# A second norm's column sums by transposes and a VectorE sum, moved into the middle of a product

## The chip, the cores and the metric

The kernel runs on one core of a Trainium2 chip. A core has a matrix engine (TensorE, PE in the profile, with its weight loads shown as PEld), a vector engine (VectorE, DVE), an activation engine (ScalarE, ACT), GpSimd (POOL) and the queues that issue DMAs (SP, and those of ACT and POOL). Each engine takes its own instructions in order, and semaphores hold an instruction back until another engine has done its part. The metric is the device time of one execution in microseconds; less is better.

## The reference

One decoder layer on a sequence of 1024 positions with a width of 1024, all in float32. Cut to what matters here:

```python
def rmsnorm(x, gain):
    y = x * lax.rsqrt(jnp.mean(x * x, axis=-1, keepdims=True) + 1e-6)
    return y * gain

h = rmsnorm(x, mix_norm)                      # first norm: its scale is also needed by the attention
x = x + merged @ w_out                        # attention, spatial gating, gates, output projection
x = x + conv_gated_mlp(rmsnorm(x, ffn_norm), w_up, conv_w, conv_b, w_down)   # second norm
```

`conv_gated_mlp` multiplies by `w_up` (1024 x 5632), applies a causal convolution of width 3, gates one half with the other and multiplies by `w_down`.

## The kernel before

All activations lie with channels on the 128 partitions and positions along the free axis. Each float32 product is made of three products of a high and a low part (`mm3` at L92 to L94, `prod` at L1127): high by high, high by low, low by high. The large products are blocked by 2 x 2 and use seven block products in place of eight, with sums of weight and activation blocks; the block names (A11, S1, T4 ...) are those of that scheme. In the up-projection a `Pair` is one gate chunk and one value chunk of 128 channels; there are 22 pairs, each of seven products of 12 matmuls, and its result lies in two PSUM tiles, `zg` (halves `g0`, `g1`) and `zv` (halves `v0`, `v1`).

**The norm's scale.** The second norm's scale is not applied to its input but to the result of the first product, since it is one number per position. Its way is:

- `square` (L1554 on) squares the new residual on ScalarE and adds the eight channel chunks on GpSimd into `sq2`, 128 partitions by 1024 positions. Its last adds are those of L1567.
- `ssq_cols` (L1747) sums `sq2` over the partitions. For each of eight groups of 128 positions, `sq2` stands as the weights and a tile `ones` of two columns is streamed, so that the sums land with positions on the partitions, in columns of `pb`, which is the still unused `zv` tile of the next pair (`q2`). VectorE copies every other column to `ss8b` (128 x 8), multiplies by 1/1024 and adds epsilon (L130), and GpSimd raises it to the power -0.5 (L131).
- `rms_rows` (L135) makes rows of that column again: for each of the eight groups one column is broadcast as the weights, and the 128 x 128 identity `ident` is streamed, so that each partition gets the scale of every position. ScalarE copies the PSUM result to `rstd_b` (L143), and VectorE multiplies with it (`scale`, L1150).

`rms_rows` is used at two places: for the first norm in the first attention step (tile `rb`, about 43 to 45 us), and for the second norm inside the second pair (about 543 to 545 us). Each is eight matmuls in the program, which the profile shows as sixteen records: a float32 matmul is recorded twice.

**The order of the work.** TensorE's order is the order of the code, for the whole kernel (a manual schedule); from the phases named here on the other engines' order is also that of the code. `first_pair` (L1843 on) runs the seven products of pair 0, and ends in the product A22·T4 into `v0`, `ssq_cols`, and then splits and sums of the next pairs' weights on GpSimd and ScalarE (`split_s3`, `sum_s2`, `sum_s4`, `adds`, which issues two DMAs from GpSimd's queue, `split_q_half`). `fast_pair(1, ...)` begins with A11·B11 of pair 1, and behind it calls `rms`: the `rms_rows` of the second norm, the scaling of pair 0, and then pair 0's convolution.

Of the kernel before, what the change touches and what calls it, by code (L numbers as in the profile page):

```python
# [10 lines left out]
F = mybir.dt.float32  # L11
# [3 lines left out]
ALU = mybir.AluOpType  # L15
AX = mybir.AxisListType
# [17 lines left out]
def build(tc, a):  # L34
    nc = tc.nc
    ctx = ExitStack()
    with ctx, tc.manual_schedule(engines={mybir.EngineType.PE}):
        body(ctx, tc, nc, a)


def body(ctx, tc, nc, a):
    L, H = slice(0, 512), slice(512, 1024)
    base = ctx.enter_context(tc.tile_pool(name="base", bufs=1))
# [28 lines left out]
    def PS(s):  # L72
        if psum.get("next"):
            return psum["next"].pop(0).tile([128, 1024], F, tag="P", name=nm(s))
        pools_ = psum["P"]
        pools_.append(pools_.pop(0))
        return pools_[-1].tile([128, 1024], F, tag="P", name=nm(s))
# [36 lines left out]
    sink_b = base.tile([128, 8], F, name="sink_b")  # L114
    ident = base.tile([128, 128], F, name="ident")
    rstd_b = base.tile([128, 1024], F, name="rstd_b")
    ones = base.tile([128, 2], F, name="ones")
    mh05 = base.tile([128, 8], F, name="mh05")
    rstd = base.tile([128, 8], F, name="rstd")
    nc.gpsimd.memset(rstd_b[:, 0:128], 1.0)  # L120
    nc.gpsimd.memset(ones, 1.0)
    nc.gpsimd.memset(mh05, -0.5)
    g2 = cp[:, 0:8]
    ng2 = sink_b
# [3 lines left out]
    def rsqrt_cols(dst, ss, n, width):  # L128

        nc.vector.tensor_scalar(dst, ss, 1.0 / width, EPS, op0=ALU.mult, op1=ALU.add)  # L130
        return nc.gpsimd.tensor_tensor(dst, dst, mh05[:, :n], op=ALU.pow)  # L131
# [3 lines left out]
    def rms_rows(pb, col, hs=(0, 1)):  # L135

        for h, p in zip(hs, pb):
            for s in range(4):
                c = 4 * h + s
                nc.tensor.matmul(p[:, s * 128:(s + 1) * 128], col[:, c:c + 1].to_broadcast([128, 128]), ident,  # L140
                                 start=True, stop=True)
        for h, p in zip(hs, pb):
            nc.scalar.copy(rstd_b[:, h * 512:(h + 1) * 512], p)  # L143

# [526 lines left out]
    def sub(eng, out, x, y, op=ALU.subtract):  # L671
        eng.tensor_tensor(out, x, y, op=op)
        return out
# [24 lines left out]
    for n in range(20):  # L698
# [12 lines left out]
        if n == 0:  # L711
            for h in (0, 1):
                rms_rows([PH("rb")], rstd, (h,))
# [252 lines left out]
    pools = {"dr": dr}  # L966
# [147 lines left out]
    class Blocks:  # L1114
# [9 lines left out]
            if self.zv is not None:  # L1124
                self.v0, self.v1 = self.zv[:, L], self.zv[:, H]

        def prod(self, o, l, r, more=False):  # L1127
            (wh, wl), y, nk = self.w[l], self.y[r], self.nk
            for k in range(nk):
                for j, (p, q) in enumerate(((wh, 0), (wh, 1), (wl, 0))):  # L1130
                    m = y[:, q, k, :] if nk == 4 else y[:, 2 * q + k, :]
                    nc.tensor.matmul(o, p[:, k, :], m, start=not more and k == 0 and j == 0,  # L1132
                                     stop=k == nk - 1 and j == 2, skip_group_check=True)
# [386 lines left out]
    def right_split(n, e, src):  # L1520

        right_split_hi(n, e, src)
        right_split_lo(n, e, src)

    def right_split_hi(n, e, src):
        copy_hi(comb_tile(n)[:, 0, 2 * e:2 * e + 2, :], src)

    def right_split_lo(n, e, src):
        t = comb_tile(n)
        ds = slice(2 * e, 2 * e + 2)  # L1530
        nc.vector.tensor_tensor(t[:, 1, ds, :], src, t[:, 0, ds, :].bitcast(F), op=ALU.subtract)
# [9 lines left out]
    def gain(n, d):  # L1541
        k = 4 * (int(n[0]) - 1) + d
        return g2[:, k:k + 1], ng2[:, k:k + 1]
# [11 lines left out]
    def square(n, e):  # L1555

        q = pools["sq2"][:, (L, H)[int(n[1]) - 1]]
        if n == "21":
            t = ob[n][:, 2 * e:2 * e + 2, :]
        else:  # L1560
            t = pools["fp"].tile([128, 2, 512], F, tag="sqt", name=nm("sqt"))
        nc.scalar.activation(t, ob[n][:, 2 * e:2 * e + 2, :], AF.Square)
        if n in ("11", "12") and e == 0:
            nc.gpsimd.tensor_tensor(q, t[:, 0, :], t[:, 1, :], op=ALU.add)
        else:
            for k in (0, 1):
                nc.gpsimd.tensor_tensor(q, q, t[:, k, :], op=ALU.add)  # L1567

    def stt(out, x, g, y, op):
        nc.vector.scalar_tensor_tensor(out, x, g, y, op0=ALU.mult, op1=op)  # L1570
# [131 lines left out]
    def a22_split():  # L1702
        w0.split(("A22",), w0.q[:, 4:8], *(wst.tile([128, 8, 128], R, tag="w" + x, name=nm("q" + x))[:, 0:4] for x in "hl"))

    def fax_split():
        fx = pools["fp"].tile([128, 4, 512], R, tag="hA", name="fax")
        w0.split(("S2", "S4"), w0.r, *(fx[:, 2 * i:2 * i + 2, :].rearrange("p a (b m) -> p (a b) m", m=128)
                                       for i in (0, 1)))
# [37 lines left out]

    def ssq_cols(p):  # L1747
        for s in range(8):
            nc.tensor.matmul(p[:, 2 * s:2 * s + 2], pools["sq2"][:, s * 128:(s + 1) * 128], ones,
                             start=True, stop=True)  # L1750
        pool = pools["fp"]
        ss = pool.tile([128, 8], F, name="ss8b")
        nc.vector.tensor_copy(ss, p[:, 0:16].rearrange("p (s two) -> p s two", two=2)[:, :, 0])
        rsqrt_cols(ss, ss, 8, D)
        return ss

# [72 lines left out]
    def first_pair():  # L1829
        w, nx = lefts[0], lefts[1]  # L1830
        pools["mr_cm"].__exit__(None, None, None)
        pools["ex"] = ctx.enter_context(tc.tile_pool(name="ex", bufs=1, side="right", reuse_waits="tile"))
        z = PS("pz"), PS("pz")
        q, q2 = Pair(0, w.w, z[::-1]), Pair(1, nx.w)
        xu = pools["fp"].tile([128, 1024], F, tag="xu", name="xu")
        x7, u2 = xu[:, L], xu[:, H]
        x1 = pools["wx"].tile([128, 512], F, tag="x1f", name="x1f")

        q.prod(q.v1, "A11", "B11")
        a22_split()  # L1840
        nc.scalar.copy(x1, q.v1)
        fax_split()
        nx.load_p()  # L1843
        nx.load_q()
        nx.load_s3()
        q.prod(q.g1, "S1", "T1")
        for e in (0, 1):
            right_split_hi("T2", e, ob["B"][:, 2 * e:2 * e + 2, :])
        for e in (0, 1):
            right_split_lo("T2", e, ob["B"][:, 2 * e:2 * e + 2, :])  # L1850
        nc.scalar.copy(u2, q.g1)
        lefts[2].load_ahead()
        q.prod(q.v0, "S3", "T3")
        square("21", 0)
        nx.adds()
        square("21", 1)
        nc.scalar.copy(x7, q.v0)
        for e in (0, 1):
            for i in (0, 1):
                d = 2 * e + i  # L1860
                p = ob["X"][e][:, i, :]
                stt(p, p, gain("21", d)[0], ob["B"][:, d, :], ALU.add)
        for e in (0, 1):
            right_split("T4", e, ob["X"][e])
        q.prod(q.g1, "S4", "B22", more=True)
        q.prod(q.g0, "A12", "B21")
        nc.vector.tensor_tensor(q.g0, q.g0, x1, op=ALU.add)
        sub(nc.vector, x7, x7, u2)
        q.prod(q.v1, "S2", "T2", more=True)
        nx.split_p()  # L1870
        q.prod(q.v0, "A22", "T4", more=True)
        pb = q2.zv
        ratio = ssq_cols(pb)
        nx.split_s3()
        nx.sum_s2()
        nx.sum_s4()
        lefts[2].adds()
        nx.split_q_half(0)
        nx.split_q_half(1)
        lefts[2].load_p()  # L1880
        nc.scalar.copy(u2, q.v1)
        q.u2 = u2
        sub(nc.vector, q.v1, x7, u2)
        sub(nc.vector, q.v0, q.v0, u2)

        def rms():

            rms_rows([pb[:, L], pb[:, H]], ratio)
            q.scale(q.zv)
            q.last_sum()  # L1890

        pools["ft_cm"] = tc.tile_pool(name="ft", bufs=1, reuse_waits="tile")
        return q, q2, rms
# [82 lines left out]
    def mlp():  # L1976
# [200 lines left out]
        def start1():  # L2177
            prep(1)
            loads(3)

        prev, q, rms = first_pair()
        for n in range(1, NPAIR):
            q = fast_pair(n, prev, q or Pair(n, lefts[n].w), (start0, start1, start), rms)
# [119 lines left out]
```

## Time and profile before

| what | value |
| --- | --- |
| time, median of 3 runs | 1157.84 us (1157.07 to 1158.2) |
| the profiled execution, its own time | 1157.13 us |
| span of its trace | 1155.4 us |
| PE busy | 1150.4 us, 100% of the span, 5789 records |
| weight loads busy | 978.1 us, 85% |
| DVE busy | 857.0 us, 74% |
| ACT busy | 588.7 us, 51% |
| POOL busy | 658.3 us, 57% |

The span runs from the first to the last recorded instruction; the 1.7 us between it and the execution's own time lie before and behind. Matmuls overlap: one matmul's recorded duration is longer than the distance to the next one's start, so TensorE's pace is read from distances of starts or from the chain of waits, not from durations. In a row of the timeline stand the start in us, the duration in us, the engine, the line, the operation, the tiles written and read with their shapes, the count of instructions merged in it, and in brackets the idle time before it with what ended it.

### The profile page before, as it was taken

The page shows a single profiled execution, that of the slowest core. Times are in us where ns is not written, and L with a number is a line of the kernel's source. Part 1 is how long each engine was busy: PE and PEld are TensorE (multiplying, and loading weights), DVE is VectorE, ACT ScalarE, POOL GpSimd, SP SyncE. Part 2 cuts the span into 40 slices and gives each one's busy share as a digit, 9 for nine tenths or more (in the row PEclk, how much of TensorE's full clock was granted, in tenths as well). Part 3 has the DMA queues.
Part 4 walks back from the last instruction along what each step waited for, and adds up shares of the span by engine and source line. Part 5 has one row for each costly group of instructions (what it writes and reads, how often), then busy time and mean ns, then how long its engine had stood idle before and what let it go on. Part 6 is the DMA issues. An engine that isn't in the chain of part 4 may idle for free.

```text
span 1155.4 us, 15810 instructions
## 1 busy us (share of the span) xinstructions
PE 1150.4 (100%) x5789; PEld 978.1 (85%) x5789; DVE 857.0 (74%) x987; ACT 588.7 (51%) x896; POOL 658.3 (57%) x461
## 2 busy tenths in 40 slices
PE   9999999999999999999999999999999999999998
PEld 9999999888888888888888888888888888888887
DVE  7787747734436889887998978797788887766664
ACT  6665568643436546686444444444444354425231
POOL 1768674598783755798877676767676730000000
PEclk9999999999999999999999999999999999999999
DMA  9443565265747766644655554645464358966571
GB/s 367 149 147 67 137 217 201 74 209 174 202 108 240 240 213 237 191 143 120 165 166 149 152 137 137 173 129 145 131 171 134 111 201 308 353 220 197 176 229 56
DMA packets 86429, 204.37 MB, mean 177 GB/s; under 512 B 9616, under 2 KB 17296, under 8 KB 86160
## 3 DMA queue, kind: packets, MB, share of 16 engines
q1 hardware_dynamic: 77280, 174.93, 43.9%
q0 software_dynamic: 8544, 19.93, 10.4%
q10 hardware_dynamic: 528, 8.52, 2.1%
q8 instruction: 45, 0.74, 0.3%
q14 instruction: 32, 0.26, 0.1%
HBM read 162.70 MB, written 57.41 MB: 191 GB/s over the span
## 4 chain that ended last, share of the span: by engine, by line
PE 93%; POOL 3%; DMA 2%; DVE 1%; issue 1%; SPq 0%; ACT 0%; POOLq 0%
PE pz L1132 56%; PE pdx L2083 9%; PE pd L2083 8%; PE pY L1723 2%; PE pX L1723 2%; POOL wjl L1591 1%; PE pu L94 1%; PE pu L92 1%; PE pu L93 1%; PE pvs L94 1%; PE pvs L92 1%; PE pvs L93 1%; PE pv L568 1%; PE pq L92 1%; PE pq L93 1%; PE pq L94 1%
## 5 line engine op out<-in xcount | busy, mean ns | idle before, releaser
L1132 PE MATMUL pz<-T,qh 128*128 128x512 f32 x464 | 143.0, 389 | 0.0
L1132 PE MATMUL pz<-B,ph 128*128 128x512 f32 x352 | 108.6, 390 | 0.0
L1132 PEld LDWEIGHTS pz<-T,qh 128*128 128x128 f32 x464 | 87.0, 188 | 18.3 <-ACT u L949 0.3
L1084 POOL TENSOR_TENSOR pl<-lp,ph 128x1024 fp32r<-128x1024 f32 x30 | 73.3, 2443 | 37.0 <-ACT ph L88 37.0
L1132 PE MATMUL pz<-T,ql 128*128 128x512 f32 x232 | 90.3, 389 | 0.0
L1150 DVE TENSOR_TENSOR pz<-pz,rstd_b 128x1024 f32<-128x1024 f32 x60 | 73.9, 1232 | 6.1 <-ACT rstd_b L143 4.1
L1132 PEld LDWEIGHTS pz<-B,ph 128*128 128x128 f32 x352 | 65.9, 188 | 13.6
L1084 POOL TENSOR_TENSOR ql<-lq,qh 128x1024 fp32r<-128x1024 f32 (+1 forms) x31 | 76.4, 2488 | 0.0
L1132 PE MATMUL pz<-T,s3h 128*128 128x512 f32 x232 | 71.4, 389 | 0.0
L1132 PE MATMUL pz<-y,wjh 128*128 128x512 f32 x224 | 69.5, 391 | 0.1
L1132 PE MATMUL pz<-B,pl 128*128 128x512 f32 x176 | 68.6, 390 | 0.1
L88 ACT ACTIVATE qh<-lq 128x1024 fp32r<-128x1024 f32 (+1 forms) x31 | 31.5, 1020 | 69.3 <-POOL pl L1084 47.4
L1084 POOL TENSOR_TENSOR s3l<-lq,s3h 128x512 fp32r<-128x512 f32 x20 | 26.0, 1301 | 65.9 <-ACT s3h L88 65.9
L1372 POOL TENSOR_TENSOR wjl<-wj,wjh 128x512 fp32r<-128x512 f32 (+1 forms) x32 | 42.0, 1332 | 35.6 <-ACT wjh L88 29.8
L1132 PE MATMUL pz<-B,AX 128*128 128x512 f32 x252 | 60.6, 389 | 0.0
L1132 PE MATMUL pz<-T,AX 128*128 128x512 f32 x252 | 60.5, 389 | 0.0
L2083 PE MATMUL pdx<-bh,ah 128*128 128x512 f32 x152 | 59.2, 390 | 0.0
L2083 PE MATMUL pdx<-bh,al 128*128 128x512 f32 x152 | 59.1, 389 | 0.0
L2083 PE MATMUL pdx<-bl,ah 128*128 128x512 f32 x152 | 59.1, 389 | 0.0
L1144 ACT COPY u<-pz 128x512 f32<-128x512 f32 x28 | 16.4, 587 | 80.8 <-DVE pz L1143 80.8
L1771 DVE SCALAR_TENSOR_TENSOR tg<-pz,cp,tg 128x1023 f32<-128x1023 f32 (+1 forms) x44 | 56.2, 1278 | 0.8
L1771 DVE SCALAR_TENSOR_TENSOR tv<-pz,cp,tv 128x1023 f32<-128x1023 f32 (+1 forms) x44 | 56.2, 1278 | 0.8
(402 smaller groups left out, 3574.6 us busy)
## 6 DMA issues: line engine op xcount, KB each, us to landing
lp<-wup SPq DMA_DIRECT2D x22, 512.0 KB, 3.8
lq<-wup SPq DMA_DIRECT2D x22, 512.0 KB, 4.1
ra<-wdown SPq DMA_DIRECT2D x44, 256.0 KB, 4.5
b<-T SPq DMA_DIRECT2D x44, 256.0 KB, 3.7
lq<-wup POOLq DMA_DIRECT2D x42, 256.0 KB, 5.1
B<-tv SPq DMA_DIRECT2D x33, 256.0 KB, 2.3
T<-tt SPq DMA_DIRECT2D x33, 256.0 KB, 2.1
b<-B SPq DMA_DIRECT2D x33, 256.0 KB, 3.0
```

The lines of the kernel that those rows point to most:

```text
L88: return nc.scalar.activation(dst, src, AF.Copy, scale=scale)
L92: nc.tensor.matmul(out, wh, mh, start=first, stop=False, **kw)
L93: nc.tensor.matmul(out, wh, ml, start=False, stop=False, **kw)
L94: nc.tensor.matmul(out, wl, mh, start=False, stop=last, **kw)
L1084: nc.gpsimd.tensor_tensor(l, r, h.bitcast(F), op=ALU.subtract)
L1132: nc.tensor.matmul(o, p[:, k, :], m, start=not more and k == 0 and j == 0, stop=k == nk - 1 and j == 2, skip_group_check=True)
L1144: nc.scalar.copy(self.u2, self.v1)
L1150: nc.vector.tensor_tensor(z, z, rstd_b, op=ALU.mult)
L1372: nc.gpsimd.tensor_tensor(l[:, k], r[:, k], h[:, k].bitcast(F), op=ALU.subtract)
L1723: nc.tensor.matmul(ob[o][e][:, d, :], p[:, 4 * d + k, :], m[:, q, k, :], start=s in (0, 5) and k == 0 and i == 0, stop=k == 3 and i == 2, ...
L1771: nc.vector.scalar_tensor_tensor(t[:, j:], p[:, 0:1024 - j], cw[:, ci, 2 - j:3 - j], t[:, j:], op0=ALU.mult, op1=ALU.add)
L2083: nc.tensor.matmul(o[d], p[:, k - k0, m], q[:, k - k0, :], start=new and k == 0 and j == 0, stop=k == HK - 1 and j == 2, skip_group_check= ...
```

## The change

Three edits.

1. In `ssq_cols` the eight matmuls with two columns of ones become eight transposes with the identity: each brings a 128 x 128 piece of `sq2` to PSUM with positions on the partitions. All 1024 columns of `pb` are written. VectorE's copy becomes a sum over each group of 128 columns (`tensor_reduce`, 128 x 1024 in PSUM to 128 x 8). The tile `ones` and its memset on GpSimd are gone; a pad of the same size keeps the places of the other tiles.
2. In `rms_rows` the eight matmuls with the identity become eight transposes of the broadcast column, at both places.
3. `ssq_cols` is called in the middle of the product A22·T4: `prod` gets a list of chunks `ks`, the first two chunks (six matmuls) run before the transposes and the last two behind. VectorE's subtraction `x7 - u2` (tile `xu`) moves from ahead of the copy to behind the sum and its scaling.

```diff
-    ones = base.tile([128, 2], F, name="ones")
+    base.tile([128, 2], F, name="pad_b")
...
-    nc.gpsimd.memset(ones, 1.0)
...
         for h, p in zip(hs, pb):
             for s in range(4):
                 c = 4 * h + s
-                nc.tensor.matmul(p[:, s * 128:(s + 1) * 128], col[:, c:c + 1].to_broadcast([128, 128]), ident,
-                                 start=True, stop=True)
+                nc.tensor.transpose(p[:, s * 128:(s + 1) * 128], col[:, c:c + 1].to_broadcast([128, 128]), ident)
...
-        def prod(self, o, l, r, more=False):
+        def prod(self, o, l, r, more=False, ks=None):
             (wh, wl), y, nk = self.w[l], self.y[r], self.nk
-            for k in range(nk):
+            for k in ks or range(nk):
...
     def ssq_cols(p):
         for s in range(8):
-            nc.tensor.matmul(p[:, 2 * s:2 * s + 2], pools["sq2"][:, s * 128:(s + 1) * 128], ones,
-                             start=True, stop=True)
+            c = slice(s * 128, (s + 1) * 128)
+            nc.tensor.transpose(p[:, c], pools["sq2"][:, c], ident)
         pool = pools["fp"]
         ss = pool.tile([128, 8], F, name="ss8b")
-        nc.vector.tensor_copy(ss, p[:, 0:16].rearrange("p (s two) -> p s two", two=2)[:, :, 0])
+        nc.vector.tensor_reduce(ss, p.rearrange("p (s d) -> p s d", d=128), axis=AX.X, op=ALU.add)
         rsqrt_cols(ss, ss, 8, D)
...
-        sub(nc.vector, x7, x7, u2)
         q.prod(q.v1, "S2", "T2", more=True)
         nx.split_p()
-        q.prod(q.v0, "A22", "T4", more=True)
+        q.prod(q.v0, "A22", "T4", more=True, ks=(0, 1))
         pb = q2.zv
         ratio = ssq_cols(pb)
+        sub(nc.vector, x7, x7, u2)
+        q.prod(q.v0, "A22", "T4", more=True, ks=(2, 3))
```

The order on TensorE, at the end of pair 0 in `first_pair`. `pz` is a PSUM tile of a product, `T` the activation block T4, `qh` and `ql` the high and low weights of A22, `sq` is `sq2`, `B` with `ph` and `pl` the first product of pair 1. Before:

```order
L1132 MATMUL pz_5436<-T_702_5514,qh_5454 128x512 x2
L1132 MATMUL pz_5436<-T_702_5514,ql_5455 128x512
L1132 MATMUL pz_5436<-T_702_5514,qh_5454 128x512 x2
L1132 MATMUL pz_5436<-T_702_5514,ql_5455 128x512
L1132 MATMUL pz_5436<-T_702_5514,qh_5454 128x512 x2
L1132 MATMUL pz_5436<-T_702_5514,ql_5455 128x512
L1132 MATMUL pz_5436<-T_702_5514,qh_5454 128x512 x2
L1132 MATMUL pz_5436<-T_702_5514,ql_5455 128x512
L1749 MATMUL pz_5439<-ones,sq_4748 128x2 x8
L1132 MATMUL pz_5438<-B_659_5112,ph_5557 128x512 x2
```

Now (line numbers are lower by two from here on, and the tile numbers by one):

```order
L1130 MATMUL pz_5435<-T_702_5513,qh_5453 128x512 x2
L1130 MATMUL pz_5435<-T_702_5513,ql_5454 128x512
L1130 MATMUL pz_5435<-T_702_5513,qh_5453 128x512 x2
L1130 MATMUL pz_5435<-T_702_5513,ql_5454 128x512
L1748 MATMUL pz_5438<-ident,sq_4747 128x128 x8
L1130 MATMUL pz_5435<-T_702_5513,qh_5453 128x512 x2
L1130 MATMUL pz_5435<-T_702_5513,ql_5454 128x512
L1130 MATMUL pz_5435<-T_702_5513,qh_5453 128x512 x2
L1130 MATMUL pz_5435<-T_702_5513,ql_5454 128x512
L1130 MATMUL pz_5437<-B_659_5111,ph_5555 128x512 x2
```

The eight instructions on `sq2` stand six matmuls earlier than before, and stream 128 columns each in place of two.

The order on VectorE at the same place. `xu` holds `x7` and `u2`, `ss8b` is the column of sums, `pz_5439` (now `pz_5438`) is `pb`. Before:

```order
L1867 TENSOR_TENSOR pz_5437<-pz_5437,x1f 128x512
L672 TENSOR_TENSOR xu<-xu 128x512
L1753 COPY ss8b<-pz_5439 128x8
L130 TENSOR_SCALAR ss8b<-ss8b 128x8
L672 TENSOR_TENSOR pz_5436<-xu 128x512
L672 TENSOR_TENSOR pz_5436<-pz_5436,xu 128x512
L1150 TENSOR_TENSOR pz_5436<-pz_5436,rstd_b 128x1024
```

Now:

```order
L1865 TENSOR_TENSOR pz_5436<-pz_5436,x1f 128x512
L1751 TENSOR_REDUCE ss8b<-pz_5438 128x8
L129 TENSOR_SCALAR ss8b<-ss8b 128x8
L670 TENSOR_TENSOR xu<-xu 128x512
L670 TENSOR_TENSOR pz_5435<-xu 128x512
L670 TENSOR_TENSOR pz_5435<-pz_5435,xu 128x512
L1148 TENSOR_TENSOR pz_5435<-pz_5435,rstd_b 128x1024
```

The subtraction within `xu` stands behind the sum and its scaling, and the copy is a reduction. On ScalarE and on the SP queue nothing moves; on GpSimd only the memset of `ones` is gone, in the kernel's first rows.

## The prediction

> **What bounds the kernel now.** I read the page first: engines, then the granted clock.
>
> ```profile
> span 1155.4 us, 15810 instructions
> PE 1150.4 (100%) x5789; PEld 978.1 (85%) x5789; DVE 857.0 (74%) x987; ACT 588.7 (51%) x896; POOL 658.3 (57%) x461
> PEclk9999999999999999999999999999999999999999
> ```
>
> TensorE is busy for the whole span at the full clock, so time can come only out of TensorE's queue or out of its few waits. Next the chain of waits around the two places that the change touches (start, duration, what), and the busy time of two long stretches (start:end, length, then busy time of PE, PEld, DVE, ACT, POOL; clock, DMA).
>
> ```profile
> 43.90 1.78 PE rb L140 x16
> ...
> 59.08 0.44 PE pt L538 x4
> ...
> 535.85 2.72 PE pz L1132 x12
> 538.57 1.68 PE pz L1749 x16
> 540.25 2.89 PE pz L1132 x12
> 543.13 1.78 PE pz L140 x16
> 544.92 397.22 PE pz L1132 x1752
> ...
> 45.00:205.00 160.00, 160.00 (x1206) 151.15 (x1205) 110.41 (x219) 106.40 (x293) 108.09 (x115) 1.00 0.50 151
> 540.08:1152.00 611.92, 611.90 (x2715) 506.70 (x2714) 478.98 (x462) 264.73 (x304) 291.97 (x171) 1.00 0.56 171
> ```
>
> All three groups that are changed lie on the chain, and behind each TensorE goes on without a gap: 160.00 of 160.00 us, and 611.90 of 611.92. So a shorter group is a gain as long as no other engine falls behind. Where that is nearest is told by TensorE's waits between the two places (in total, times, longest):
>
> ```profile
> PEld pz L1132 <- POOL pl L1084: 0.5, 1, 0.5
> PEld pz L1132 <- ACT x L1392: 0.5, 2, 0.3
> PEld pz L1132 <- DVE y L1306: 0.5, 1, 0.5
> ```
>
> They are half a microsecond each, and what they wait for is itself fed by TensorE's results (the chain goes back from each of them to TensorE).
>
> **The change part by part.** *The price of a transpose.* The trace has float32 transposes of the same size: four of them (L538) take 0.44 us of the chain above, 0.11 each, and their 64 are recorded once each:
>
> ```profile
> L538 PE MATMUL pt<-ident,c x64: 270/272/273, 58.9 to 158.9; 128*128 128x128 f32 x64
> ```
>
> *`rms_rows`, two places.* Sixteen records, 1.78 us each time. Eight transposes at 0.11 are 0.88 us. TensorE gains 0.90 at each.
>
> *`ssq_cols`.* Sixteen records, 1.68 us; eight transposes are again 0.88, a gain of 0.80. Together TensorE's queue gets 0.90 + 0.80 + 0.90 = 2.60 us shorter. There is up to 0.17 more: the twelve matmuls ahead of the second `rms_rows` took 2.89, while those of A22 took 2.72, and part of that may be a wait for the power on GpSimd (below), which ended at 542.79 while the load that needs it began at 542.84. I leave this 0.17 to the range.
>
> The page "TensorE: Matmul & The Clock Gate" of the Trainium skill, Part 4, speaks against the edit: it gives about 275 ns for a transpose inside a kernel. The trace agrees with that as a recorded duration (272 ns), not as the distance at which transposes follow each other (110 ns); by the page's figure 24 transposes would be an estimated 6.6 us.
>
> *The DVE sum and the way to the scale.* What must be early is the scale's chain. These are its rows (timeline), with rows for the price of a reduction:
>
> ```profile
> 540.29 0.17 DVE L1753 COPY ss8b<-pz 128x8 f32<-128x8 f32 x1 [1.18 <-PE pz L1749]
> 540.49 0.17 DVE L130 TENSOR_SCALAR ss8b<-ss8b 128x8 f32<-128x8 f32 x1
> 540.57 0.69 DVE L672 TENSOR_TENSOR pz<-xu 128x512 f32<-128x512 f32 x1
> 540.74 2.05 POOL L131 TENSOR_TENSOR ss8b<-ss8b,mh 128x8 f32<-128x8 f32 x1 [2.18 <-DVE ss8b L130]
> 542.84 1.89 PEld L140 LDWEIGHTS pz<-ident,ss8b 128*128 128x128 f32 x16
> 27.85 0.67 DVE L372 TENSOR_REDUCE kss<-ksq 128x8 f32<-128x512 f32 x1
> 30.06 0.42 DVE L331 TENSOR_REDUCE qss<-qsq 128x4 f32<-128x256 f32 x1
> 546.07 1.23 DVE L1150 TENSOR_TENSOR pz<-pz,rstd_b 128x1024 f32<-128x1024 f32 x1 [4.07 <-ACT rstd_b L143]
> ```
>
> A reduction of 512 took 0.67 and of 256 0.42: 0.25 more for 256. For 1024 that is 0.67 + 2 x 0.25 = 1.17; the 1024-wide operation on PSUM took 1.23. I take 1.20 (bounds 1.15 and 1.30). Now the places: A22's six first matmuls end at 535.85 + 2.72/2 = 537.21, the transposes at 538.09, VectorE begins 0.04 later as it did behind L1749 (540.25 to 540.29), so 538.13, sums until 539.33, and the scaling by 1/1024 starts at 539.36, where it stood at 540.49: 1.13 us earlier. To this comes the 0.90 of the first place, if it lasts: 2.03 in all.
>
> The power on GpSimd is next. It took 2.05 here and between 1.64 and 2.59 elsewhere:
>
> ```profile
> 28.72 1.22 DVE L241 CUSTOM_DVE_ANT_0 xt<-xt 128x1024 f32<-128x1024 f32 x1
> 28.89 2.59 POOL L381 TENSOR_TENSOR krs<-krs,mh 128x8 f32<-128x8 f32 x1 [25.19 <-DVE krs L378]
> 35.32 1.64 POOL L381 TENSOR_TENSOR krs<-krs,mh 128x8 f32<-128x8 f32 x1
> ```
>
> The longest ran beside a DVE operation with two inputs from SBUF, the 1.64 beside none. The 2.05 ran beside the subtraction at 540.57, which reads two halves of `xu`. After the change the subtraction `x7 - u2` stands at that same place, right behind the scaling, and has two such inputs too. So I keep 2.05; 1.64 would bring 0.41, 2.59 would cost 0.54.
>
> *Does TensorE then wait for the scale?* It comes to the second `rms_rows` at 537.21 + 0.88 + 1.36 + 2.72 = 542.17 by the chain's ends, which is 0.96 before its 543.13; the scale is there 1.13 before. No wait.
>
> *Edits at no cost.* The transposes need `sq2`:
>
> ```profile
> 532.85 3.35 POOL L1567 TENSOR_TENSOR sq<-sq,ac 128x512 f32<-128x512 f32 x2
> 536.15 2.40 POOL L1084 TENSOR_TENSOR pl<-lp,ph 128x1024 fp32r<-128x1024 f32 x1
> 536.82 0.41 PEld L1132 LDWEIGHTS pz<-T,qh 128*128 128x128 f32 x2
> ```
>
> The adds end at 536.20, and the load that the transposes replace began at 536.82: 0.62 us of cover; what the adds lose beyond it, TensorE waits. The subtraction in `xu` moves from 536.35 to about 539.4; the next user of `xu` needs a ScalarE copy of 539.48, itself up to 0.88 later since A22 ends later. The two subtractions then end near 542, ahead of the scaling of pair 0, which waits for `rstd_b` until about 543. The memset that is gone lies in the first microseconds, under the first loads.
>
> *What is late next.* Behind the power GpSimd goes on without a pause, and ScalarE and VectorE follow from it:
>
> ```profile
> 545.33 1.29 POOL L672 TENSOR_TENSOR lr<-lp,lr 128x512 f32<-128x512 f32 x1
> 546.57 0.94 POOL L1042 DMA_DIRECT2D lq<-wup  x1
> 552.89 0.63 ACT L88 ACTIVATE s3h<-lq 128x512 fp32r<-128x512 f32 x1 [1.87 <-DMA lq<-wup]
> 554.38 1.01 ACT L1791 ACTIVATE pz<-tg 128x1024 f32<-128x1024 f32 x1
> 555.41 1.23 DVE L1794 SCALAR_TENSOR_TENSOR pz<-pz,tg 128x1024 f32<-128x1024 f32 x1 [0.65 <-ACT pz L1791]
> ...
> 595.56 0.68 DVE L672 TENSOR_TENSOR x<-x,pz 128x512 f32<-128x512 f32 x1
> 596.48 0.86 PE L1132 MATMUL pz<-B,AX 128*128 128x512 f32 x3
> ```
>
> The adding DMA is issued behind `lr` in GpSimd's queue; ScalarE waits for its landing, and behind this split stand the next one and pair 0's tanh, for which VectorE waits. All of them come earlier only as much as the power does, 2.03 us, not 2.60. VectorE then has hardly a pause for two pairs. The product S4·B22 of pair 3 overwrites the PSUM half that the subtraction at 595.56 reads; it ends at 596.24, and TensorE starts at 596.48: 0.24 of slack. So TensorE keeps at most 2.03 + 0.24 = 2.27 there, and I forecast that about 0.35 of the 2.60 is lost at this place.
>
> **The sum.** 2.27, rounded to 2.25. The profiled execution would go from 1157.13 (span 1155.4) to 1154.9. That execution was 0.7 below the median of the runs; against the median of 1157.84 the same gain gives 1155.6.
>
> **The rivals.**
>
> *A, all of TensorE's gain arrives*: the power gets shorter (1.64), or the adding DMA lands sooner, and VectorE keeps up. For it: VectorE's wait of 4.07 us ahead of the scaling. Against it: 0.24 us of slack at 596. 1157.84 - 2.60 = 1155.2; with the 0.17, 1155.1.
>
> *B, the first place brings nothing*: in the attention steps VectorE and ScalarE work in a loop with TensorE, and ScalarE's copy of `rb` came 0.35 us behind other work of its own rather than early:
>
> ```profile
> 45.26 0.20 ACT L507 COPY c<-nsink 128x4 f32<-128x4 f32 x1 [1.02 <-DVE vhl L425]
> 45.61 0.59 ACT L143 COPY rstd_b<-rb 128x512 f32<-128x512 f32 x1
> ```
>
> If the 0.90 is waited away before 205 us, 1.35 remains: 1156.5. Against it: TensorE was busy for 160.00 of the 160.00 us behind that place, so nothing there was late yet.
>
> *C, slower, by the rate of transposes*: if each of the 24 occupied TensorE for its recorded 0.272 us, as it might where none of them can overlap the next one's load, they would take 6.53 against the 1.78 + 1.68 + 1.78 = 5.24 that go: 1.29 more, 1159.1. It decides from 0.218 us a transpose on. Against it: 0.44 for four, in a row of the chain. By the page of the Trainium skill named above (its 275 ns as a rate) the result would be this rival's, and the trace's 110 ns speaks against it.
>
> *D, the change doesn't do what it says*: a transpose of a broadcast column is still recorded twice, so that `rms_rows` stays as it is, and only the 0.80 at `ssq_cols` is left of TensorE's gain: 1157.0.
>
> **How the numbers follow.** Forecast 0.50, A 0.18, B 0.18, C 0.06, D 0.08. The forecast's own bounds: a reduction of 1.30 and a power of 2.59 take 0.1 + 0.54 from it (1156.3), a power of 1.64 adds up to 0.35 (1155.2). The range, 1154.6 to 1157.2, holds these, A, B and D, with half a microsecond for the median of three runs (they lay 1.1 apart), and leaves out C. Faster or slower is told from no change by 0.2%, which is 2.3 us here: below 1155.5 is faster. The forecast stands almost on that edge, so a little under half of it (0.23) counts as faster, with most of A (0.16) and a trace of B (0.03): 0.42. Slower is C, 0.06. The rest is 0.52.
>
> **What would show it.** Each changed group should be 0.85 to 0.95 us in TensorE's chain, with eight records; 1.7 or sixteen records mean D, over 2 means C. The reduction should last 1.15 to 1.30, and the power 2.05 beside a subtraction in `xu`; if it lasts 1.64, A gains. TensorE's waits should show one for VectorE's L670 near 574 or 594 us, of 0.1 to 0.4 us: without it A was right. If TensorE at 205 us is not 0.9 earlier than before (measured at the last product of the attention phase), B was right. The forecast is wrong if the transposes wait for `sq2`, which a wait of TensorE for L1565 (the former L1567) would show.

## The result, and the profile after

The change brings 0.2%: the median falls from 1158.02 us (1157.05 to 1160.14, 12 runs) to 1155.42 us (1154.89 to 1156.48, 12 runs), a ratio of 0.998 with a 95% interval of 0.9973 to 0.9987. That is 2.6 us less by the medians, between 1.5 and 3.1 by the interval. Run twice more beside the kernel before, as controls of the experiments below, it gave 0.998 (0.9971 to 0.9989) and 0.9976 (0.9967 to 0.9986), or 2.2 and 2.5 us. The forecast was a gain of 2.25 and 1155.6 us.

The profiled execution of the change took 1156.18 us, 0.95 less than that of before. Its page, the span, the engines and the granted clock:

```profile
span 1154.4 us, 15760 instructions
PE 1148.8 (100%) x5765; PEld 975.6 (85%) x5765; DVE 852.5 (74%) x987; ACT 588.4 (51%) x896; POOL 658.5 (57%) x460
PEclk9999999999999999999999999999999999999999
```

TensorE is still busy all the time, at the full clock, with 24 records fewer: eight in place of sixteen at each of the three groups. The groups themselves, in the timeline of the change (start, duration, engine, line, operation, tiles, count; in brackets the idle time before), with the work on the scale's chain between them:

```profile
537.20 1.03 PE L1748 MATMUL pz<-ident,sq 128*128 128x128 f32 x8
537.99 0.71 PE L1130 MATMUL pz<-T,qh 128*128 128x512 f32 x2
538.27 1.23 DVE L1751 TENSOR_REDUCE ss8b<-pz 128x8 f32<-128x1024 f32 x1 [1.73 <-PE pz L1748]
539.53 0.17 DVE L129 TENSOR_SCALAR ss8b<-ss8b 128x8 f32<-128x8 f32 x1
539.61 0.68 DVE L670 TENSOR_TENSOR xu<-xu 128x512 f32<-128x512 f32 x1
539.78 2.05 POOL L130 TENSOR_TENSOR ss8b<-ss8b,mh 128x8 f32<-128x8 f32 x1 [0.71 <-DVE ss8b L129]
542.16 1.03 PE L139 MATMUL pz<-ident,ss8b 128*128 128x128 f32 x8
543.00 0.72 PE L1130 MATMUL pz<-B,ph 128*128 128x512 f32 x2
```

Eight transposes take 0.79 and 0.84 us from their first start to that of the next matmul, which itself is about 0.1 slower than usual. The power on GpSimd ends at 541.83, and the transposes that need it start at 542.16, at TensorE's own pace. Now the chain of waits, with the first group and the place where it leaves TensorE again (start, duration, what):

```profile
45.02 0.87 PE rb L139 x8
...
539.78 2.05 POOL ss8b L130
541.83 1.25 POOL s3l L1082
...
545.64 7.25 DMA lq<-wup
...
575.41 0.60 DVE x L670
576.02 0.04 issue
576.07 19.34 PE pz L1130 x84
```

Before, the chain from 544.92 on was one piece of TensorE, 397.22 us long. Now it comes to TensorE at 576.07, from a VectorE subtraction, and that goes back over the adding DMA to the power. The waits and the two long stretches (start:end, length, then busy time of PE, PEld, DVE, ACT, POOL; clock, DMA) say how much this is:

```profile
PEld pz L1130 <- DVE x L670: 0.9, 2, 0.5
PEld pk L390 <- DVE kr L383: 0.7, 1, 0.7
```

```profile
45.00:205.00 160.00, 160.00 (x1206) 151.14 (x1203) 111.37 (x221) 106.64 (x294) 108.08 (x115) 1.00 0.50 151
540.08:1152.00 611.92, 610.83 (x2703) 504.97 (x2702) 478.07 (x462) 265.34 (x307) 291.71 (x171) 1.00 0.56 172
```

In the second stretch TensorE is now idle for 1.09 of 611.92 us, where it was 0.02. The first stretch has no gap, as before.

**Where two executions start apart.** The second of these waits is not the change's. It lies at 33 us, behind the first loads, and these landed later in this execution than in that of before. The chains' first pieces, before:

```profile
5.81 11.53 DMA xr<-xw
...
28.89 2.60 POOL krs L381
```

and after:

```profile
5.33 13.18 DMA xr<-xw
...
30.06 2.60 POOL krs L379
```

The loads are the same in both kernels; one took 1.65 us longer here. What TensorE does from there on is 1.2 us late before any changed instruction of its own has run. So a single trace of the change can't be held against a single trace of before by its span. What can is the shift of the same TensorE instruction (its start in the one trace less its start in the other), read behind each place and counted from the one at 41 us. The table has this for every kernel run below, each against the trace of before, in us (minus is earlier). Where nothing is changed, between 46 us and the second norm, a shift still moves by up to 0.25, so smaller differences between two traces say little.

| kernel | 41 us, ahead of `rb` | 46, behind `rb` | 546, behind the second `rms_rows` | 578, pair 2 | 597, pair 3 | 1140 |
| --- | --- | --- | --- | --- | --- | --- |
| the change | +1.22 | +0.21 | -1.66 | -1.25 | -0.96 | -0.98 |
| the change again (e5) | +0.48 | -0.52 | -2.28 | -2.20 | -1.97 | -1.96 |
| the change, third (e10) | +0.53 | -0.48 | -2.34 | -2.32 | -2.04 | -2.03 |
| `rms_rows` alone (e1) | +0.42 | -0.59 | -1.51 | -0.58 | -0.30 | -0.30 |
| `ssq_cols` alone (e2) | +0.37 | +0.37 | -0.83 | -0.83 | -0.72 | -0.71 |
| first place alone (e8) | +0.12 | -0.89 | -0.75 | -0.75 | -0.79 | -0.80 |
| transposes behind A22 (e3) | +0.40 | -0.51 | -1.35 | -1.09 | -0.80 | -0.79 |
| subtraction first (e7) | +1.42 | +0.51 | -0.84 | +0.32 | +0.60 | +0.57 |
| subtraction first, again (e9) | +0.34 | -0.67 | -2.32 | -2.07 | -1.82 | -1.81 |
| adding DMAs early (e4) | +0.32 | -0.69 | -2.55 | -2.55 | -2.59 | -2.57 |
| adding DMAs early, again (e6) | +0.36 | -0.65 | -2.28 | -2.28 | -2.32 | -2.35 |

In the three traces of the change TensorE gains 2.88, 2.76 and 2.87 by 546 us (1.01 of it between 41 and 46 us, around `rb`), gives back 0.70, 0.31 and 0.31 at pairs 2 and 3, and keeps 2.20, 2.44 and 2.56 to the end.

**What gives it back.** These are the rows from the adding DMA to the late product in the trace of the change (timeline):

```profile
545.64 0.93 POOL L1040 DMA_DIRECT2D lq<-wup  x1
552.97 0.63 ACT L88 ACTIVATE s3h<-lq 128x512 fp32r<-128x512 f32 x1 [3.52 <-DMA lq<-wup]
553.68 1.29 POOL L1082 TENSOR_TENSOR s3l<-lq,s3h 128x512 fp32r<-128x512 f32 x1 [1.28 <-ACT s3h L88]
555.50 1.23 DVE L1792 SCALAR_TENSOR_TENSOR pz<-pz,tg 128x1024 f32<-128x1024 f32 x1 [1.88 <-ACT pz L1789]
558.02 2.92 DVE L670 TENSOR_TENSOR tt<-tv 128x512 f32<-128x512 f32 x1
558.45 1.94 POOL L670 TENSOR_TENSOR lr<-lq,lp 128x512 f32<-128x512 f32 x1
594.69 0.68 DVE L670 TENSOR_TENSOR x<-x,pz 128x512 f32<-128x512 f32 x1
595.42 2.34 PE L1130 MATMUL pz<-B,AX 128*128 128x512 f32 x9
```

and the rows of before, in the same view, that the prediction didn't show:

```profile
553.60 1.30 POOL L1084 TENSOR_TENSOR s3l<-lq,s3h 128x512 fp32r<-128x512 f32 x1 [0.27 <-ACT s3h L88]
555.23 0.89 POOL L1042 DMA_DIRECT2D lq<-wup  x1 [0.34 <-issue]
556.72 0.86 POOL L1043 DMA_DIRECT2D lq<-wup  x1 [0.60 <-DMA lq<-wup]
557.94 3.87 DVE L672 TENSOR_TENSOR tt<-tv 128x512 f32<-128x512 f32 x1
559.65 1.60 POOL L672 TENSOR_TENSOR lr<-lq,lp 128x512 f32<-128x512 f32 x1
576.20 0.68 DVE L672 TENSOR_TENSOR x<-x,pz 128x512 f32<-128x512 f32 x1
577.43 2.88 PE L1132 MATMUL pz<-B,AX 128*128 128x512 f32 x12
```

Three things are to be seen. First, VectorE waits for the tanh (1.88 us), and the chain view, which follows waits on semaphores, leads that way; but that is not what sets VectorE's pace: the subtraction `tt` behind it, which reads two operands from SBUF, lasts 2.92 us, far longer than the 0.68 of its kind, and ends 0.55 after GpSimd's `lr` has ended (560.94 and 560.39). Before, it lasted 3.87 and ended 0.56 after `lr` (561.81 and 561.25). Second, from there on VectorE, with the ScalarE work that it waits for, is without slack: its subtraction `x` in pair 3 stands 0.87 earlier than before, `lr`'s end 0.86. Third, S4·B22 of pair 3 starts 0.05 after that subtraction ends (595.37), where it had 0.24 before. At pair 2 the slack before was 577.43 - 576.88 = 0.55; VectorE's round from one `x` to the next takes 19.36 us (576.20 to 595.56), TensorE's 19.05 (577.43 to 596.48), and so 0.31 of it goes from one pair to the next.

### The profile page after: what moved, and what is told of

Read it like the earlier page. It is cut to its first block, busy times and chain, and to the rows that moved or that the text cites. A ratio compares the mean times of both kernels' runs of the same rounds, so it can differ in the third digit from the quotient of the medians.

```text
span 1154.4 us, 15760 instructions
## 1 busy us (share of the span) xinstructions
PE 1148.8 (100%) x5765; PEld 975.6 (85%) x5765; DVE 852.5 (74%) x987; ACT 588.4 (51%) x896; POOL 658.5 (57%) x460
## 4 chain that ended last, share of the span: by engine, by line
PE 90%; DVE 3%; POOL 3%; DMA 2%; ACT 1%; issue 0%; SPq 0%; POOLq 0%; ACTq 0%
PE pz L1130 51%; PE pdx L2082 9%; PE pd L2082 8%; PE pY L1721 3%; PE pX L1721 2%; PE pu L94 1%; PE pu L92 1%; PE pvs L94 1%; PE pu L93 1%; PE pvs L92 1%; PE pvs L93 1%; PE pv L566 1%; DMA xr<-xw 1%; PE pq L92 1%; PE pq L93 1%; PE pq L94 1%
```

## The experiments

The theory: TensorE's queue becomes shorter at all three places, but what is kept is bounded by the chain from the column sums over the power and the adding DMA to VectorE's `x`, so that the parts don't add up, the place of the transposes within A22 matters, and an earlier adding DMA gives the rest. Its rivals: the gain is TensorE's queue alone, wherever the transposes stand; the first place brings nothing; the wait for `x` has another cause than the adding DMA. Each kernel ran in five rounds beside the kernel before, which had medians of 1157.75 (e1 to e4), 1157.96 (e5 to e8) and 1157.63 (e9 and e10).

### Each half alone (e1, e2)

e1 is the kernel before with this edit only (both places):

```diff
-                nc.tensor.matmul(p[:, s * 128:(s + 1) * 128], col[:, c:c + 1].to_broadcast([128, 128]), ident,
-                                 start=True, stop=True)
+                nc.tensor.transpose(p[:, s * 128:(s + 1) * 128], col[:, c:c + 1].to_broadcast([128, 128]), ident)
```

> Only the transposes of the broadcast column at both places; the squares are summed as before, behind A22. Theory 1 (what is kept is the smaller of two gains: what TensorE's queue gets shorter, and what the way to the scale gets earlier, plus 0.24 to 0.35 us of slack at S4.B22 of pairs 2 and 3): TensorE's queue is 1.8 us shorter, the way to the scale is earlier only by the first place's 0.9, so 1.15 to 1.25 us below before, and TensorE waits about 0.6 us for VectorE's subtraction x between 570 and 600 us. Theory 2 (all that leaves TensorE's queue arrives): 1.8 us below before and no such wait.

Measured: 1156.80, ratio 0.9994 (0.9985 to 1.0003), 0.95 us less by the medians.

e2 is the change without this edit:

```diff
-                nc.tensor.transpose(p[:, s * 128:(s + 1) * 128], col[:, c:c + 1].to_broadcast([128, 128]), ident)
+                nc.tensor.matmul(p[:, s * 128:(s + 1) * 128], col[:, c:c + 1].to_broadcast([128, 128]), ident,
+                                 start=True, stop=True)
```

> Only the second norm's sum by transposes in the middle of A22; rms_rows as before with matmuls at both places. Theory 1: TensorE's queue is 0.8 us shorter, the way to the scale 1.1 us earlier, so all of the 0.8 arrives, and no wait for the subtraction x near 570 to 600 us. Theory 2: 0.8 us as well; this run gives the term by itself, and with e1 tells whether the parts add up (theory 1: e1 and e2 together give 2.0, less than the whole change, since each lacks what the other brings; theory 2: they give the whole change).

Measured: 1157.15, ratio 0.9992 (0.9984 to 1.0001), 0.60 us less. The two halves make 1.55 by the medians, the whole 2.2 to 2.6. Intervals of some 1 us either way don't show that the difference is real; the traces say why it should be. In e1 TensorE gains 1.93 by 546 us (+0.42 to -1.51) and then waits for `x`, in total, times, longest:

```profile
PEld pz L1131 <- DVE x L671: 1.4, 2, 1.0
```

Only 0.72 stays, since nothing in e1 but the first place makes the scale's chain earlier. That is less than the 1.15 to 1.25 expected, and the wait is twice the 0.6: the adding DMA took 7.6 us to land in this trace where it took 6.2 before. In e2 the power starts at 539.76 in place of 540.74, and TensorE gains 1.20 (0.95 of it from the start of A22 to the end of `rms_rows`, the rest ahead of that, where nothing is changed). The expectation had no wait for `x` here; one of 0.3 came, and 1.08 is left. Each half moves one side of the bound; the whole moves both.

### The first place alone (e8)

The kernel before, with the transposes only where `rms_rows` is called for the first norm:

```diff
+                if len(hs) == 1:
+                    nc.tensor.transpose(p[:, s * 128:(s + 1) * 128], col[:, c:c + 1].to_broadcast([128, 128]), ident)
+                else:
```

> Only the first norm's eight transposes (tile rb), all else as before. Theory 1: TensorE's queue is 0.9 us shorter there, and all other engines follow, since TensorE has no wait behind it until 205 us: 0.9 us below before at every later product, and 0.9 in the time. Rival B of the prediction: the attention loop takes it back, and nothing of it is left at 205 us.

Measured: 1156.72, ratio 0.9988 (0.9979 to 0.9997), 1.24 us less. In the trace TensorE gains 1.01 around `rb`; 0.95 of it is there at 205 us, and 0.92 at the end. The rival that the attention phase takes the first gain back falls.

### The transposes behind all of A22 (e3)

The change, with its transposes in the place where the matmuls stood before:

```diff
-        q.prod(q.v0, "A22", "T4", more=True, ks=(0, 1))
+        q.prod(q.v0, "A22", "T4", more=True)
...
-        q.prod(q.v0, "A22", "T4", more=True, ks=(2, 3))
```

> The whole change, but the eight transposes of the squares stand behind A22, where the matmuls with ones stood. TensorE's queue is as short as in the change (2.6 us less). Theory 1: the way to the scale starts 1.36 us (six matmuls) later than in the change, so it is 0.2 us later than before at this place and 0.7 earlier with the first place's gain; TensorE waits for the scale ahead of the second transposes (about 1 us) and again for VectorE's subtraction x, and only 0.9 to 1.1 us of gain is left. Theory 2: the place does not matter, 2.6 us below before, like the change.

Measured: 1156.87, ratio 0.9991 (0.9982 to 1.0), 0.88 us less: 1.3 to 1.7 are lost against the change. The waits of its trace:

```profile
PEld pz L139 <- POOL ss8b L130: 1.3, 1, 1.3
PEld pz L1130 <- DVE x L670: 0.6, 2, 0.4
```

The power starts at 540.39 rather than 539.16 (e5), and TensorE's weight load waits 1.3 us for it, which holds its matmuls back by 1.08. The transposes stand 1.36 later (half of A22, 2.72 / 2). In the trace 1.19 us are kept, where the change kept 2.20 to 2.56. So TensorE's shorter queue alone isn't the gain; the place of the transposes is about half of it.

### The change again, and the adding DMAs ahead of the power (e5, e4, e6)

e5 is the change itself, beside e6.

> The change itself once more, unaltered, beside the next runs. Theory 1: 2.0 to 2.6 us below before, and a second trace shows TensorE waiting again for VectorE's subtraction x at S4.B22 of pairs 2 and 3, 0.3 to 0.9 us in all, with the first adding DMA behind lr taking over 7 us from issue to landing (7.25 in the first trace, 6.24 in the trace of before). If that landing time was chance in one execution, the wait is 0.35 us or less, as the rows of before gave.

Measured: 1155.75, ratio 0.998. Its trace has one wait for `x`, 0.4 us at pair 3, and the DMA landed in 6.8 us: less than the 7 that were expected, and still more than the 6.2 of before.

e4 and e6 are one kernel: the change, with the call that issues the two adding DMAs moved ahead of the column sums, so that in GpSimd's queue they stand ahead of the power, not behind it:

```diff
         q.prod(q.v0, "A22", "T4", more=True, ks=(0, 1))
+        lefts[2].adds()
         pb = q2.zv
         ratio = ssq_cols(pb)
...
-        lefts[2].adds()
```

> The change, and the two adding DMAs of pair 2's weights are issued from GpSimd's queue ahead of the power instead of behind the sums lr. Theory 1a (what holds TensorE back at S4.B22 is the landing of this DMA: in the trace of the change it was issued 0.93 us earlier than before and landed at the same time, 552.9): ScalarE's split s3h no longer waits at 552.9, tanh and VectorE's chain are over 1 us earlier, TensorE's waits for x vanish, and 0.4 to 0.7 us come on top of the change: 2.6 to 3.2 us below before. Theory 1b (VectorE's own length between the scaling and pair 3 is the bound): waits for x stay, and the time is that of the change. GpSimd's power may be up to 1 us later by the two issues in front of it, which would show as a wait ahead of the second transposes.

> The change with the two adding DMAs ahead of the power, once more, against the change in the same job. Theory 1a: no wait for x, the adding DMAs land 4 to 5.5 us behind their issue, and the time is 0.3 to 0.7 us below that of the change. Theory 1b: equal times.

Measured: 1155.13 in e4 and 1155.00 in e6, both with a ratio of 0.9975 (0.9966 to 0.9984 and 0.9965 to 0.9984); in e6 that is 0.75 below the change in the same comparison. In the timeline of e4:

```profile
537.75 0.88 POOL L1040 DMA_DIRECT2D lq<-wup  x1
538.34 1.19 POOL L1041 DMA_DIRECT2D lq<-wup  x1
538.96 2.28 POOL L130 TENSOR_TENSOR ss8b<-ss8b,mh 128x8 f32<-128x8 f32 x1
554.73 1.94 POOL L670 TENSOR_TENSOR lr<-lq,lp 128x512 f32<-128x512 f32 x1
556.11 1.12 DVE L670 TENSOR_TENSOR tt<-tv 128x512 f32<-128x512 f32 x1
```

The wait for `x` is gone from both traces, and what TensorE has at 546 us it has at the end (-2.55 and -2.57; -2.28 and -2.35). `tt` lasts 1.12 here, and still ends 0.56 after `lr` (557.23 and 556.67): with the DMA early it is `lr` that has moved, by 4.58. The power takes 2.28 rather than 2.05 (why isn't shown; here it stands right behind the two issues), and TensorE's weight load waits 0.3 for it at the second `rms_rows`, which holds its matmuls back by 0.04 at most. The cause of the wait for `x` is the adding DMA's place in GpSimd's queue, and this order is the best of the kernels run, though its interval overlaps that of the change.

### The subtraction back at its old place (e7, e9, e10)

The change moved `x7 - u2` behind the scaling. e7 and e9 are the change with that one call back:

```diff
+        sub(nc.vector, x7, x7, u2)
         q.prod(q.v1, "S2", "T2", more=True)
...
-        sub(nc.vector, x7, x7, u2)
```

> The change, but VectorE's subtraction x7 - u2 stands where it stood before, ahead of the sum. In the trace of before it took 2.76 us, until GpSimd's long split pl had ended, and so the sum queued behind it starts about 1.3 us later than in the change. Theory 1: the scale is later by that, TensorE waits 1.0 to 1.3 us for it ahead of the second transposes, and the time is 0.8 to 1.3 us above the change. Rival: the order of two VectorE operations off the chain does not matter; the time is that of the change.

Measured: 1156.15, ratio 0.9986 (0.9977 to 0.9995), 0.40 above the change. Its trace had begun 1.42 late, and waited 1.4 us for `x`; so it was run again beside the change:

> The kernel of e7 once more, beside the change. In e7 the trace lost 1.3 to 1.5 us against the traces of the change (TensorE waited 0.5 us for the power and 1.4 us for x), but the medians lay only 0.4 us apart. If the trace of e7 was a typical execution: waits for the power of 0.3 to 0.6 and for x of 0.7 to 1.4 us again, medians 0.8 to 1.5 us above the change. If it was an unlucky one: waits for x under 0.7 us and medians 0.3 to 0.6 us above.

> The change for the third time, as the measure for e9: 2.0 to 2.6 us below before, TensorE's wait for x between 0.3 and 0.9 us in its trace.

Measured: 1155.72, ratio 0.9985 (0.9976 to 0.9994), against 1155.09 for the change. The old place costs 0.4 to 0.6 us by the medians, whose intervals overlap, and 0.41 by the traces of e9 and e10; that is less than expected. The trace of e7 was an unlucky one: the adding DMA took 7.7 us to land, and in e9 6.75. In the timeline of e7:

```profile
537.09 2.76 DVE L670 TENSOR_TENSOR xu<-xu 128x512 f32<-128x512 f32 x1
536.90 2.39 POOL L1082 TENSOR_TENSOR pl<-lp,ph 128x1024 fp32r<-128x1024 f32 x1
539.77 1.21 DVE L1751 TENSOR_REDUCE ss8b<-pz 128x8 f32<-128x1024 f32 x1
541.26 1.67 POOL L130 TENSOR_TENSOR ss8b<-ss8b,mh 128x8 f32<-128x8 f32 x1 [1.97 <-DVE ss8b L129]
541.73 0.70 DVE L670 TENSOR_TENSOR pz<-xu 128x512 f32<-128x512 f32 x1 [0.54 <-ACT xu L1880]
```

The subtraction, now beside GpSimd's `pl`, lasts 2.76 us, ends 0.56 after `pl` (539.85 and 539.29) and holds the reduction back; but the power lasts 1.67 rather than 2.05. It isn't that no such subtraction runs beside it: the next one (`pz<-xu`, also two operands from `xu`) begins 0.47 into the power and lasts its usual 0.70. In the traces with 2.05 a subtraction of this kind was already under way, 0.17 ahead, when the power began. In e9 it is 1.67 too:

```profile
539.79 1.67 POOL L130 TENSOR_TENSOR ss8b<-ss8b,mh 128x8 f32<-128x8 f32 x1 [1.97 <-DVE ss8b L129]
```

So the move is worth what it saves in front of the reduction less the 0.38 that it costs by starting just ahead of the power.

### One rule for all traces

The end of `lr` (its row's start plus duration), the end of `x` in pair 3 and TensorE at 1140 us, each against before, in us:

| kernel | `lr` ends | `x` ends | TensorE at the end | wait for `x` |
| --- | --- | --- | --- | --- |
| the change | -0.86 | -0.87 | -0.98 | 0.9 |
| e5 | -1.91 | -1.89 | -1.96 | 0.4 |
| e10 | -1.96 | -1.96 | -2.03 | 0.4 |
| e1 | -0.20 | -0.20 | -0.30 | 1.4 |
| e2 | -0.66 | -0.65 | -0.71 | 0.3 |
| e3 | -0.70 | -0.70 | -0.79 | 0.6 |
| e7 | +0.71 | +0.69 | +0.57 | 1.4 |
| e9 | -1.75 | -1.73 | -1.81 | 0.4 |
| e8 | -1.01 | -0.99 | -0.80 | none |
| e4 | -4.58 | -4.32 | -2.57 | none |
| e6 | -4.34 | -4.03 | -2.35 | none |

Wherever TensorE waits for `x`, it ends where `x` puts it, within 0.06 to 0.12, and `x` where `lr` puts it, within 0.02. Where it doesn't wait, it ends with what its own queue gained.

## Why the prediction was right

**The price of a transpose** was taken at 0.11 us, eight at 0.88. The chain has 0.87 for the eight of `rb`, and their count is eight. The recorded duration stayed at 0.27 us, so the distance was the right reading; rivals C (the duration as the rate, slower) and D (still two records) fall with these rows.

**TensorE's queue** was to be 2.60 shorter with up to 0.17 more; the three traces show 2.88, 2.76 and 2.87. By the distances from each group's first start to the next matmul's, the groups give 0.91 (1.70 to 0.79), 0.91 (1.70 to 0.79) and 0.87 (1.70 to 0.84), 2.69 in all. The 0.17 was not a wait of TensorE for the power, as the prediction thought possible: before, the first matmul of the second `rms_rows` starts 0.23 behind the one ahead of it, the usual distance. Most of it is the slow matmul behind the column sums (0.32 to the next start), and such a one is still there after the change. What the shifts show above 2.69 lies outside the groups, and its cause is open.

**The reduction** was set at 1.20 within 1.15 and 1.30 and took 1.23. The scaling was to be 1.13 earlier by the move alone: 539.53 for 540.49 is 0.96, in a trace that was 0.14 late at that place, so 1.10. The **power** was kept at 2.05 because the subtraction beside it reads two operands from SBUF, with 1.64 for a free one; it took 2.05. The reason was half right: in e7 and e9 such a subtraction also ran beside the power, which took 1.67, so by the rows what counts is that it is under way when the power begins. **No wait at the second `rms_rows`**: none is in the traces of the change. **No wait for `sq2`**: none for L1565. The cover was 0.62 in the prediction. In the first trace it was 0.25 (GpSimd's adds ended at 536.72 and the first load began at 536.97), in e5 and e10 0.61 and 0.65.

**The first place** was taken as kept (rival B, 0.18, said not), and e8 shows it; in the traces of the change the gain at 205 us is 0.90 to 0.99. **All of the gain** (rival A) does not arrive: in each trace of the change TensorE waits for L670.

**What is late next.** The place (S4·B22 of pair 3) and the source (the adding DMA behind the power) were right, and the size came out close: 0.35 to be lost, 0.31 lost in two of the three traces and 0.70 in the first. The way there was not right, and this is the step that failed: the prediction led the delay over ScalarE's split and the tanh to VectorE, and assumed that the DMA would land as much earlier as it was issued, 2.03. It was issued that much earlier (546.57 to 545.02 in e5 is 1.55, with the 0.48 at the start 2.03), but it took longer to land. The DMA view has each of the two (issue, operation, count, KB, us to landing), before:

```profile
lq<-wup POOLq DMA_DIRECT2D x1, 256.0 KB, 6.2
```

and after:

```profile
lq<-wup POOLq DMA_DIRECT2D x1, 256.0 KB, 7.2
```

In e5 and e10 it was 6.8. What was lost there came back further on: VectorE isn't bound by the tanh but by the end of GpSimd's `lr`, and GpSimd had waited 0.34 and 0.60 us at its next DMAs before, which it doesn't after. From the issue of the adding DMA to the end of `lr` it is 14.68 before and 14.75, 14.32 and 14.32 in the traces of the change. So two errors of the chain's middle, about +0.6 to +1.0 for the landing and -0.94 for the waits, cancelled in the first trace and left the chain 0.36 earlier in the other two. Against that, less of the 0.24 of slack was to be had (in e5 and e10 TensorE's shift at the end goes only 0.07 beyond that of `x`), and TensorE's queue was shorter by 0.16 and 0.27 more than the 2.60. That the loss came to 0.31 is therefore partly luck: the errors happened to balance. The first trace lost more at pair 3 (and waited at pair 2 too) since its DMA landed latest of the three.

**The sum.** 2.25 was forecast; the traces kept 2.20, 2.44 and 2.56, the medians 2.6, 2.2 and 2.5. The profiled execution was forecast at 1154.9 and took 1156.18: the working had no term for executions that begin late, and this one did by 1.2. The question of faster or no change was left nearly even, at 0.2%; three measurements of 0.20, 0.20 and 0.24% by ratio stand on that same edge. (One sum of the prediction is off in its last digit: its slower bound, 1155.6 and 0.64, makes 1156.2 and not 1156.3.)

## What to carry to other kernels

Where TensorE bounds, price an added operation by the distance at which its kind starts in the trace, not by its recorded duration, and then ask how much earlier the other engines' chain gets that feeds the next reuse of a buffer: the smaller of the two is what stays. That chain is to be followed over operations that look merely slow, for a VectorE subtraction of 3 to 4 us with two inputs in SBUF was in truth held by GpSimd. And a DMA issue that needs nothing from a waiting instruction belongs ahead of it in the queue: here that gave about 0.3 us more of the gain in the traces.

## What the runs showed of the hardware

**VectorE held by GpSimd.** In all twelve traces `tt`, which has two inputs in SBUF, ends 0.56 us after GpSimd's `lr`, whether it had started 0.4 before it (e5), 1.7 before (the kernel before) or 1.4 behind it (e4); its recorded time goes from 1.10 (e6) to 3.96 us (e2) with that. The subtraction in `xu` ends the same 0.56 after `pl` in e7. The Trainium skill, page "SBUF — State Buffer", section "Who interferes with whom", says that a VectorE instruction with two inputs from SBUF contends with a GpSimd instruction that reads SBUF, that the pair of ports they share is an exclusive lock, and that the order of issue decides which of the two is blocked. The traces agree for `tt` and for the power, which is 0.38 longer when a subtraction had begun 0.17 ahead of it (2.05 and 1.67); but a subtraction that begins 0.47 into the power (e7) lasts 0.70, as if it were alone. That `tt` stays held although `lr` starts behind it, by the rows, they show too; whether GpSimd's instruction ahead (`pl`) hands on the hold or its recorded end is rough, no run here tells.

**The landing of an adding DMA.** With 256 KB it landed 4.0 us after its issue in e4, where only the second adding DMA was issued near it and SP issued no load, and 6.2 to 7.7 us in the place behind `lr`, where SP issues its loads within the same microsecond. Before, SP's last of these was issued at 548.89, 2.3 us behind; in the change it comes 0.9 us behind the adding DMA (546.57), and the landing is the slower one. In the ten traces with the DMA at that place, the landings of 6.2 to 6.5 (the kernel before, e2, e8) go with an SP load that stayed 1.5 to 1.8 us in its queue, and those over 6.7 with loads that took 0.4 there. In these seven `lr` ends 7.48 to 7.50 us after the landing; in the three, where GpSimd then waits at its next DMAs, 7.90 to 8.54. So a late landing goes through to `lr` in full, and an early one is used up by other waits: from issue to the end of `lr` it is 14.2 to 15.2 us in all ten. What makes the landing late wasn't tried.

**The start of an execution.** TensorE at 41 us stood between 0.12 and 1.42 us later than in the trace of before in eleven executions. In the change that comes from the first loads. In e7, the latest, the trace shows no wait of TensorE between 5 and 41 us: its first 192 matmuls (`pkv`) take 23.8 us from the first start to the last, where before they took 22.1, at a granted clock of 1.00 in both. Why they came more slowly is open. This is as large as most effects here, and a trace's span says less than its shifts.
